# A decoder trunk on one core: where the second half's q is kept, and when its attention is queued

## The chip, the cores and the metric

One core of a Trainium2 chip runs the whole program. The metric is device time in microseconds (us) from launch to end. The engines are PE (TensorE, matmul and its weight loads), DVE (VectorE), ACT (ScalarE), POOL (GpSimd) and SP (SyncE, which here only issues DMAs). Each engine runs its instructions in the order in which they stand in its own queue; between engines they wait on semaphores.

## The reference

Two layers over x of 1024 tokens by 1024 features, float32. The first has the mixer that the change touches: one input projection feeds a sliding-window attention with rotary positions and a gated delta rule; both outputs, side by side, go through an output projection, and a layernorm and an MLP follow. The second layer has a recurrent mixer and the same MLP.

```python
def hybrid_mixer(x, w_in, sinks, conv_w, a_log, dt_bias, norm_w, w_out):
    proj = x @ w_in
    qa, ka, va, qkv_b, z, beta_logit, a_logit = split_cols(proj, HYB_SPLITS)
    qa = apply_rope(qa.reshape(bsz, T, A_Q_HEADS, A_HEAD_DIM))
    ka = apply_rope(ka.reshape(bsz, T, A_KV_HEADS, A_HEAD_DIM))
    o_a = sliding_window_attention(qa, ka, va, sinks)
    qkv_b = jax.nn.silu(causal_dwconv(qkv_b, conv_w))
    ...
    o_b = gated_delta_rule(qb, kb, vb, g, beta)
    ...
    return jnp.concatenate([o_a, o_b], axis=-1) @ w_out
for layer in range(DEPTH):
    x = layer_norm(DN_ALPHA * x + mix, ln1_g[layer], ln1_b[layer])
    x = layer_norm(DN_ALPHA * x + sqrelu_mlp(x, mlp_w1[layer], mlp_w2[layer]), ln2_g[layer], ln2_b[layer])
```

## The kernel before, in words

The 1024 tokens are two halves of 512 (`c` = 0 and 1, the first and the second half), each four tiles of 128 (`NT`). A float32 product is made of three matmuls in a reduced float32 format: every operand is kept as two parts, `h` (rounded) and `l` (what is left), and `mm3` adds h·h, h·l and l·h. Weights come by DMA to a staging tile `ws` and are split into `wh` and `wl` (`wblock`: a cast, mostly on ACT, and a subtract on DVE). Activations that are inputs of a product lie in an `ActT`: four tiles of 128x2048 for 512 features by 512 tokens each, two of parts h, two of parts l. `oT` is the `ActT` of the mixer's output; its features 0 to 511 (`quad(0, n)` for token tile n) are the attention's, the others (`oT.h(4 + h)`) those of delta head h.

The tiles of 128x2048 come from one pool of 14 (`gran`, ring `g`); `need("g", n)` holds a generator until n of them are free. There are smaller rings `t`, `s` and `f` of 128x512. PSUM has 8 banks: 4 for projections (`mm`), 4 for the small chains (`mx`).

The order of the program is made in Python by generators. `stream(c)` emits the heavy projections of half c: `hybrid` (the mixer's input projections: `kv_proj`, `q_proj`, and for delta head h `head_front` for k, q, v and `head_z` for the gate), `mix_out` (the output projection `out_proj`, with the layernorm behind it), `mlp_ln`, then the second layer. `mixers` is a list of small generators: `attn_preps` (rotary and transposes for one token tile after another), `attention` (scores, softmax, product with v), `head_mid` (the delta rule's chain of one head: four levels of a triangular solve in 32x32 blocks, then a scan over four token tiles), `layernorm`. The loop at the end keeps a clock of its own: when a mixer is due, it is advanced by a step, otherwise the current stream is, by one group of three matmuls. A stream that yields `UNIT` gives up its turn, and the loop picks again, the stream of lower phase first, the first half before the second; one that yields nothing special stays. PE's order is exactly the order in which the loop emits; the other engines' is made by a scheduler from it.

What matters around the change:
- `q_proj` puts q of half c into a tile of the pool, `st["qg"]`; `attn_preps` gives it back after its fourth `attn_prep`.
- `oT.quad(0, n)` takes the two tiles of the attention's output when it is first called, which `q_proj` does.
- The first half's `mix_out` needs two free tiles for the sums `yg`. `load_x(1)`, which loads and splits x of the second half, needs four.
- The second half's delta heads run one at a time: it has one ring, `t`.
- `mlp` takes the hidden blocks of the first layer in pairs of `straight` (4 blocks of 128 columns each) as long as the second half's `out_proj` has not begun, asked at every second one; from then on by `seven`, which makes a 2x2 block product with 7 products in place of 8, from sums of weights that POOL's and SP's DMAs prepare (`w2_sums`).

Of the kernel before, what the change touches and what calls it, by code (L numbers as in the profile page):

```python
# [13 lines left out]
ALU = mybir.AluOpType  # L14
# [6 lines left out]
CH = 512  # L21
# [27 lines left out]
BLOCK, UNIT = "block", "unit"  # L49
# [164 lines left out]
def trunk(ctx: ExitStack, tc, I, out):  # L214
    nc = tc.nc
    clk = Clock(tc, nc)
    V, G, S, PE = clk.engine(nc.vector, "V"), clk.engine(nc.gpsimd, "G"), clk.engine(nc.scalar, "S"), clk
# [14 lines left out]
    def nm(s):  # L232
        uid[0] += 1
        return f"{s}_{uid[0]}"
# [4 lines left out]
    def take(r, t):  # L239
        rings[r] -= 1  # L240
        assert rings[r] >= 0, r
        clk.tag[t.name] = r
        if spare[r]:
            old = min(spare[r], key=clk.touch)
            spare[r].remove(old)
            clk.reuse(t, old)
        return t

    def gran(dt=F32):
        return take("g", gpool.tile([P, 2048], dt, tag="g", name=nm("g")))  # L250
# [4 lines left out]
    def ts(r, dt=F32):  # L255
        return tl(r, dt)[:, :512]

    def free(r, *tiles):
        rings[r] += len(tiles)
        spare[r] += [t.name for t in tiles]  # L260
        assert rings[r] <= (GB if r == "g" else RINGS[r])

    def need(r, n=1):
        return wait(lambda: rings[r] >= n)
# [4 lines left out]
    def wait(cond):  # L269
        while not cond():  # L270
            yield BLOCK
# [4 lines left out]
    def mx_ps():  # L276
        return clk.tile("mx", 4, pmx.tile([P, 512], F32, tag="mx", name=nm("mx")))

    def v4(a):
        return a.rearrange("p (a b) -> p a b", a=4)  # L280
# [113 lines left out]
    def split_ps(h, l, ps):  # L394
        S.copy(h, ps)
        V.tensor_tensor(l, ps, h, ALU.subtract)
# [26 lines left out]
    def proj_tm(srcs, x, n, nk=KT, pre=None):  # L423
        ps = [mm_ps() for _ in range(NT)]
        for k2, src in enumerate(srcs):
            if pre is not None:
                pre(k2)
            wh, wl = wblock(src, 2 * n)
            for j in range(2):
                k = 2 * k2 + j  # L430
                for t in range(NT):
                    a, b = t * P, (t + 1) * P
                    mm3(ps[t][:, :n], x.h(k, a, b), x.l(k, a, b), wh[j], wl[j], k == 0, k == nk - 1)
                    if not (k == nk - 1 and t == NT - 1):
                        yield
        return ps
# [322 lines left out]

    def q_proj(c, x, st, oT):  # L760
        ps = yield from proj_tm([I["hin_q"][i] for i in range(4)], x, 512)
        st["qg"] = gran()
        for n in range(NT):
            oT.quad(0, n)
            S.copy(st["qg"][:, n * CH:(n + 1) * CH], ps[n])
        yield UNIT

    def kv_proj(c, x, st, oT, pre):
        ps = yield from proj_tm([I["hin_kv"][i] for i in range(4)], x, 264, pre=pre)
        st["ba"] = cpool.tile([P, NT, 8], F32, tag="ba", name=nm("ba"), bufs=2)  # L770
        st["k"] = []
        st["v"] = []
        for n in range(NT):
            kr = cpool.tile([P, P], F32, tag="kraw", name=nm("kraw"), bufs=5)
            v = cpool.tile([P, P], F32, tag="vraw", name=nm("vraw"), bufs=7)
            st["k"].append(kr)
            S.copy(st["ba"][:, n, :], ps[n][:, 256:264])
            S.copy(st["k"][n], ps[n][:, :128])
            S.copy(v, ps[n][:, 128:256])
            st["v"].append(v)  # L780
        yield UNIT

    def rope(x, src, ng, n, a, b):
        nh = x.shape[2] // 32
        cs, sn = (angles["t"].rearrange("p (s t d) -> p s t d", s=2, d=32)[:, k, n:n + 1, :].unsqueeze(1)
                  .to_broadcast([P, ng, nh, 32]) for k in range(2))
        av, bv = (z.rearrange("p (g h d) -> p g h d", g=ng, d=32) for z in (a, b))
        xv = src.rearrange("p g (h d) -> p g h d", d=32)
        V.tensor_tensor(av, xv, cs, ALU.mult)
        V.tensor_tensor(bv, xv, sn, ALU.mult)  # L790
        x4 = x.rearrange("p g (h s d) -> p g h s d", s=2, d=32)
        a4, b4 = (z.rearrange("p (g h s d) -> p g h s d", g=ng, s=2, d=32) for z in (a, b))
        V.tensor_tensor(x4[:, :, :, 0, :], a4[:, :, :, 0, :], b4[:, :, :, 1, :], ALU.subtract)
        V.tensor_tensor(x4[:, :, :, 1, :], a4[:, :, :, 1, :], b4[:, :, :, 0, :], ALU.add)

    def attn_prep(c, n, st, tl, o):
        q, kr = v4(st["qg"][:, n * CH:(n + 1) * CH]), st["k"][n]
        yield from need("f", 2)
        a, b, qs = tl[n % 2], ts("f"), v4(ts("f"))
        rope(kr.unsqueeze(1), kr.unsqueeze(1), 1, n, a[:, :128], b[:, :128])  # L800
        rope(qs, q, 4, n, a, b)
        yield at(kr, qs)
        ps = mx_ps()
        PE.transpose(ps[:, :P], kr, ident)
        kT = cpool.tile([P, P], F32, tag="kT", name=nm("kT"), bufs=4)
        V.tensor_copy(kT, ps[:, :P])
        ps = mx_ps()
        for g in range(4):
            PE.transpose(ps[:, g * P:(g + 1) * P], qs[:, g, :], ident)
        free("f", b, qs)  # L810
        S.copy(a, ps)
        o["qT"], o["kT"] = a, kT
        yield at(a, kT)
        o["ok"] = True
# [395 lines left out]
    def spawn(g, t=0.0):  # L1210
        mixers.append([lambda: t, g])

    def slots(n):
        slot["g"] = [gran() for _ in range(n // 4)]
        return [g[:, i * 512:(i + 1) * 512] for g in slot["g"] for i in range(4)]

    y2 = [dpool.tile([CH, D], F32, name=f"y2_{c}", tag=f"y2_{c}") for c in range(2)]
    st = [dict(), dict()]
    slot = dict(tl=None)

    def attn_preps(c, st, o):
        yield from wait(lambda: c == 0 or sts[0].get("att") == 4)
        angles["t"] = clk.tile("angles", 1, cpool.tile([P, 256], F32, tag="angles", name=nm("angles")))
        DA.dma_start(angles["t"], I["angles"][c])
        for n in range(NT):
            yield from wait(lambda: st.get("att", 0) >= n - 1)
            yield from attn_prep(c, n, st, slot["tl"], o[n])
        free("g", st["qg"])

    def attention(c, st, oT, o):  # L1230
        for n in range(NT):
            yield from attn_block(c, n, st, oT, slot["tl"], o[n])
            st["att"] = n + 1
        if c == 1:
            free("g", *slot["g"])
# [10 lines left out]
    def hybrid(c, x, oT, st, rs):  # L1246
        d = [dict() for _ in range(4)]
        if c == 0:
            slot["tl"] = slots(8)
            yield from kv_proj(c, x, st, oT, lambda k2: load_xT(c, x, k2))  # L1250
            DS.dma_start(csb, I["consts"])
        else:
            yield from wait(lambda: "x" in st)
            yield from head_front(c, 0, x, d[0], rs[0])
            yield from wait(lambda: sts[0].get("att", 0) >= 2)
            yield from kv_proj(c, x, st, oT, None)
        spawn(delta_scalars(c, st))

        def q():
            yield from need("g", 3)  # L1260
            yield from q_proj(c, x, st, oT)
            o = [dict() for _ in range(NT)]
            spawn(attention(c, st, oT, o))
            spawn(attn_preps(c, st, o))
        par = len(rs) > 1
        if not par:
            yield from q()
        for h in range(4):
            if h or par:
                yield from head_front(c, h, x, d[h], rs[h % len(rs)])  # L1270
            if not par and h:
                if h == 1:
                    yield from wait(lambda: "ln0" in sts[0])
                    yield from need("g", 2)
                yield from head_z(h - 1, x, oT, d[h - 1])
            yield from wait(lambda: h - st.get("scan", 0) < len(rs))
            spawn(head_mid(c, h, st, d[h], oT, rs[h % len(rs)]))
            if h == 1 and par:
                yield from q()
                yield from need("g", 2)  # L1280
                yield from head_z(0, x, oT, d[0])
                yield from head_z(1, x, oT, d[1])
                spawn(load_x(1, xTs[1]))
        if par:
            yield from head_z(2, x, oT, d[2])
        yield from head_z(3, x, oT, d[3])
        x.free()
        yield from wait(lambda: st.get("mids") == 4 and st.get("att") == 4)
# [215 lines left out]
```

## Time and profile before

| | |
|---|---|
| median of 3 runs | 2280.9 us (2277.67 to 2282.2) |
| the profiled execution | 2280.57 us, span 2278.7 us |
| mean granted clock of TensorE | 0.991 |
| instructions | 31,897 |
| first half's mixer, its input projections | to about 197 us |
| second half's kv and q projections | 245.3 to 290 us |
| first half's output projection | 365.0 to 425.1 us |

How to read it: busy time of PE overstates its pace, since matmuls overlap in the records; the distance between the starts of two neighbours is what one costs. In the tables of windows a column shows the busy time of an engine and how many of its instructions lie in the window; the granted clock is a share of full speed. In a timeline, the number in brackets is the engine's idle time before the row, and what ended it. Names such as `mm` and `mx` are PSUM tiles, `g`, `t`, `s`, `f` tiles of the rings; a matmul that reads `wh` or `wl` is a projection.

### The profile page before, as it was taken

To read this page: it belongs to the slowest core of one execution; us is meant where nothing else is said; L and a number is where in the kernel's file an instruction comes from. 1 tells how busy PE (TensorE), PEld (TensorE's weight loads), DVE (VectorE), ACT (ScalarE), POOL (GpSimd) and SP (SyncE) were. 2 spreads that over 40 slices of the span, in tenths; PEclk is the share of its full clock that TensorE was granted. 3 is DMA by queue.
4 is the path that set the end of the run, shared out by engine and by line. 5 is a ranking of instruction groups with operands and counts; after the bars stand their busy time and mean duration, and the time that the engine had idled before them with its cause. 6 is when DMAs were issued, how large, how long until landed. Compare 5 with 4: busy or idle time off the path is not lost.

```text
span 2278.7 us, 31897 instructions
## 1 busy us (share of the span) xinstructions
PE 2216.7 (97%) x12436; PEld 1790.4 (79%) x12436; DVE 1545.9 (68%) x2809; ACT 1049.1 (46%) x1874; POOL 28.9 (1%) x56
## 2 busy tenths in 40 slices
PE   8999989999999999999999999999999999999997
PEld 7767866778878887888888878878788887888886
DVE  7787684766645666596567898685565656776477
ACT  5465444434332344454344577373434444444442
POOL 0000000000000000000000000000000000000000
PEclk9999999999999999999999999999999999999999
DMA  4121221266778666677764343322533443454341
GB/s 165 61 78 39 94 67 45 74 175 178 216 213 225 196 211 200 210 241 229 226 216 149 128 138 105 136 79 97 180 107 121 139 148 123 155 166 148 120 163 69
DMA packets 87064, 332.22 MB, mean 146 GB/s; under 512 B 9600, under 2 KB 9984, under 8 KB 78720
## 3 DMA queue, kind: packets, MB, share of 16 engines
q1 hardware_dynamic: 73808, 275.32, 35.2%
q0 software_dynamic: 4608, 33.56, 7.8%
q10 hardware_dynamic: 8496, 21.30, 2.7%
q8 instruction: 97, 1.59, 0.3%
q14 instruction: 55, 0.45, 0.1%
HBM read 321.75 MB, written 75.50 MB: 174 GB/s over the span
## 4 chain that ended last, share of the span: by engine, by line
PE 85%; DVE 9%; ACT 3%; DMA 1%; issue 1%; ACTq 0%; DVEq 0%; SPq 0%
PE mm L206 66%; PE mx L206 17%; DVE g L178 3%; DVE wl L178 2%; PE mx L210 2%; DVE s L178 1%; DMA ws<-w 1%; ACT g L178 1%; ACT wh L178 1%; ACT s L178 1%; DVE t L178 1%; DVE f L178 1%; ACT f L178 0%; ACT t L178 0%; DVE lnw L178 0%
## 5 line engine op out<-in xcount | busy, mean ns | idle before, releaser
L206 PE MATMUL mm<-g,wh 128*128 128x512 f32 x2816 | 883.7, 395 | 3.6 <-DVE g L178 3.0
L178 DVE TENSOR_TENSOR wl<-ws,wh 128x1024 fp32r<-128x1024 f32 (+1 forms) x444 | 538.3, 1212 | 396.1 <-ACT wh L178 391.8
L178 ACT CAST wh<-ws 128x1024 fp32r<-128x1024 f32 (+1 forms) x356 | 371.5, 1044 | 705.8 <-PE mm L206 605.3
L206 PEld LDWEIGHTS mm<-g,wh 128*128 128x128 f32 x2816 | 521.6, 188 | 113.4 <-DVE g L178 5.1
L206 PE MATMUL mm<-g,wl 128*128 128x512 f32 x1408 | 549.5, 390 | 0.5 <-DVE wl L178 0.5
L206 PE MATMUL mm<-wh,s 128*128 128x512 f32 x1152 | 376.6, 393 | 0.7 <-DVE g L178 0.7
L206 PEld LDWEIGHTS mm<-g,wl 128*128 128x128 f32 x1408 | 264.7, 188 | 57.0 <-DVE wl L178 1.0
L206 PEld LDWEIGHTS mm<-wh,s 128*128 128x128 f32 x1152 | 216.3, 188 | 46.7 <-ACT s L178 1.1
L206 PE MATMUL mm<-wh,g 128*128 128x512 f32 (+1 forms) x768 | 239.3, 383 | 6.6 <-ACT wh L178 6.4
L206 PE MATMUL mm<-wl,s 128*128 128x512 f32 x576 | 224.3, 389 | 0.0
L206 PE MATMUL mx<-wh,s 128*128 128x512 f32 x576 | 187.8, 392 | 1.2 <-DVE s L178 1.2
L206 PEld LDWEIGHTS mm<-wh,g 128*128 128x128 f32 x768 | 143.0, 191 | 33.8 <-ACT wh L178 6.4
L178 ACT CAST s<-g 128x512 fp32r<-128x512 f32 x172 | 104.7, 622 | 105.2 <-PE mm L206 53.7
L178 DVE TENSOR_TENSOR s<-g,s 128x512 fp32r<-128x512 f32 x172 | 116.1, 685 | 44.7 <-ACT s L178 44.7
L206 PE MATMUL mm<-wl,g 128*128 128x512 f32 (+1 forms) x384 | 144.1, 375 | 0.2 <-DVE wl L178 0.2
L206 PEld LDWEIGHTS mx<-wh,s 128*128 128x128 f32 x576 | 108.1, 188 | 24.1 <-DVE s L178 2.0
L206 PEld LDWEIGHTS mm<-wl,s 128*128 128x128 f32 x576 | 108.3, 188 | 20.9
L206 PE MATMUL mx<-wl,s 128*128 128x512 f32 x288 | 112.1, 389 | 0.0
L178 DVE CAST wh<-ws 128x1024 fp32r<-128x1024 f32 x88 | 60.4, 686 | 73.0 <-PE mm L206 66.3
L178 DVE TENSOR_TENSOR g<-g,mm 128x512 f32<-128x512 f32 x136 | 89.1, 682 | 14.6 <-PE mm L206 14.2
L178 ACT ACTIVATE g<-mm 128x512 f32<-128x512 f32 x100 | 59.3, 593 | 73.0 <-PE mm L206 73.0
L206 PEld LDWEIGHTS mm<-wl,g 128*128 128x128 f32 x384 | 73.3, 191 | 11.7 <-DVE wl L178 0.6
(231 smaller groups left out, 2401.3 us busy)
## 6 DMA issues: line engine op xcount, KB each, us to landing
ws<-w SPq DMA_DIRECT2D x232, 512.0 KB, 3.3
ws<-t SPq DMA_DIRECT2D x96, 512.0 KB, 3.3
t<-w POOLq DMA_DIRECT2D x32, 1024.0 KB, 9.1
ws<-hin_fm SPq DMA_DIRECT2D x32, 512.0 KB, 3.3
t<-w SPq DMA_DIRECT2D x16, 1024.0 KB, 6.7
t<-t SPq DMA_DIRECT2D x16, 1024.0 KB, 6.5
ws<-rin SPq DMA_DIRECT2D x32, 512.0 KB, 3.3
ws<-hout SPq DMA_DIRECT2D x16, 512.0 KB, 3.4
```

The costliest lines, as they stand in the source:

```text
L178: r = f(*a, **k)
L206: ins = self.pe.matmul(out, lhsT, rhs, start=start, stop=stop, skip_group_check=fresh)
L210: return self._pe(self.pe.transpose(out, x, ident), out, [x], 0.00042 * 2 * out.shape[-1])
```

## The change

For the second half alone, q no longer gets a tile of its own. `q_proj` writes it as two parts, h and l, into the two tiles of `oT` that will take the attention's output of the same token tile; `attn_prep` adds them into its scratch tile and applies the rotary there. The second half's `q` then needs two free tiles, not three. For both halves, the `yield UNIT` at the end of `q_proj` goes, and a `yield UNIT` stands behind the spawn of each `head_mid`: attention, its preps and the delta head are in the list of mixers before the loop picks a stream again.

```diff
     def q_proj(c, x, st, oT):
         ps = yield from proj_tm([I["hin_q"][i] for i in range(4)], x, 512)
-        st["qg"] = gran()
+        g = st["qg"] = gran() if c == 0 else None
+        st["q"] = []
         for n in range(NT):
-            oT.quad(0, n)
-            S.copy(st["qg"][:, n * CH:(n + 1) * CH], ps[n])
-        yield UNIT
+            h, l = oT.quad(0, n)
+            if g is None:
+                split_ps(h, l, v4(ps[n]))
+                st["q"].append((h, l))
+            else:
+                S.copy(g[:, n * CH:(n + 1) * CH], ps[n])
+                st["q"].append(v4(g[:, n * CH:(n + 1) * CH]))
...
     def attn_prep(c, n, st, tl, o):
-        q, kr = v4(st["qg"][:, n * CH:(n + 1) * CH]), st["k"][n]
+        q, kr = st["q"][n], st["k"][n]
         yield from need("f", 2)
         a, b, qs = tl[n % 2], ts("f"), v4(ts("f"))
         rope(kr.unsqueeze(1), kr.unsqueeze(1), 1, n, a[:, :128], b[:, :128])
+        if c:
+            V.tensor_tensor(qs, *q, ALU.add)
+            q = qs
         rope(qs, q, 4, n, a, b)
...
-        free("g", st["qg"])
+        if c == 0:
+            free("g", st["qg"])
...
         def q():
-            yield from need("g", 3)
+            yield from need("g", 3 - c)
             yield from q_proj(c, x, st, oT)
...
             spawn(head_mid(c, h, st, d[h], oT, rs[h % len(rs)]))
+            yield UNIT
             if h == 1 and par:
                 yield from q()
```

The change is small, what it does to the order is not: the order is made by the loop, and from the first head on every choice can fall otherwise. Three places of it follow. The first is PE's queue behind the last matmul of the second half's q projection (`mm<-wh`). `mm_3370<-g` is `head_front` of delta head 1, the `mx` rows are the first steps of `head_mid` of head 0. Before:

```order
L206 MATMUL mm_3116<-wh_3317,g_2006 128x512
L206 MATMUL mm_3370<-g_2003,wh_3366 128x512
L206 MATMUL mm_3370<-g_2004,wh_3366 128x512
L206 MATMUL mm_3370<-g_2003,wl_3367 128x512
L210 MATMUL mx_3394<-csb,t_2285 128x128 x4
L210 MATMUL mx_3404<-csb,t_2578 128x128 x4
L206 MATMUL mx_3428<-t_3387,csb 128x512
```

Now, at the same place, with `mm_3431<-wh` and `mm_3432<-wh` the first half's `out_proj`:

```order
L206 MATMUL mm_3160<-wh_3326,g_2200 128x512
L210 MATMUL mx_3385<-csb,t_2592 128x128 x4
L210 MATMUL mx_3395<-csb,t_2789 128x128 x4
L206 MATMUL mx_3419<-t_3378,csb 128x512
L206 MATMUL mm_3431<-wh_3437,g_1079 128x512
L206 MATMUL mm_3431<-wl_3438,g_1079 128x512
L206 MATMUL mm_3431<-wh_3437,g_1080 128x512
L206 MATMUL mm_3432<-wh_3437,g_1079 128x512
```

The first half's `out_proj` moved up from 374 instructions behind that projection to 9 behind it; `head_front` of head 1 moved behind `out_proj`, and the first half's layernorm and the first block of its MLP follow it. From the end of `out_proj` to that first block PE's queue has 72 weight matmuls, where before, from the same to the same, it had 120.

The second place is PE's queue in the first half, where the triangular solve of its delta heads 2 and 3 (32x32 blocks, `t` of head 2 and `s` of head 3) lies beside its last attention tile and `head_front` of the second half (`mm_2292<-g`). Before, a piece of it:

```order
L206 MATMUL mx_2265<-t_1788 32x32 x16
L206 MATMUL mm_2292<-g_2003,wh_2288 128x512
L206 MATMUL mm_2292<-g_2004,wh_2288 128x512
L206 MATMUL mm_2292<-g_2003,wl_2289 128x512
L206 MATMUL mx_2253<-g_147,vraw_315 64x512
L210 MATMUL mx_2297<-csb,g_146 128x128 x2
L210 MATMUL mx_2297<-csb,g_147 128x128 x2
L206 MATMUL mx_2303<-t_1788 32x32 x16
```

Now, the end of the same stretch, up to the first matmul of that `head_front`:

```order
L206 MATMUL mx_2436<-s_2094 32x32 x16
L206 MATMUL mx_2454<-t_1765 32x32 x16
L206 MATMUL mx_2478<-t_1765 32x32 x16
L206 MATMUL mx_2497<-s_2094 32x32 x16
L206 MATMUL mx_2516<-t_1765 32x32 x16
L206 MATMUL mx_2534<-s_2094 32x32 x16
L206 MATMUL mx_2552<-t_1765 32x32 x16
L206 MATMUL mx_2571<-s_2094 32x32 x16
L206 MATMUL mm_2599<-g_2197,wh_2595 128x512
```

Where groups of three weight matmuls stood between the steps, 241 instructions in a row now have none; `head_front` of the second half begins 220 instructions later.

The third place is ACT's queue in the first half's MLP, behind its sixteenth hidden block (a `straight` has `r<-mm`, a block for `seven` has `g<-mm`; `lnw` rows are the second half's layernorm, `wh` casts are weights). Before:

```order
L178 ACTIVATE g_7179<-g_7179,lnw_7341 128x512 x3
L178 CAST wh_7624<-ws_7622 128x1024
L178 ACTIVATE g_7180<-g_7180,lnw_7341 128x512 x4
L178 ACTIVATE g_7553<-mm_7561 128x512
L178 ACTIVATE g_7553<-g_7553 128x512
```

Now:

```order
L178 CAST wh_7371<-ws_7369 128x1024
L178 ACTIVATE r_7250<-mm_7211 128x512
L178 ACTIVATE t_6576<-mx_7255,hsc_6574 128x128
L178 ACTIVATE r_7250<-r_7250 128x512
L178 CAST s_7197<-r_7250 128x512
```

Eight hidden blocks (two `straight`) more are made in full form, and one `seven` of the first layer's first half is gone: over the program, `mm<-wh,t` and `mm<-wl,t` products of 128x512 grow by 96, `mx<-wh,s` and `mx<-wl,s` fall by 72. On DVE there are 7 instructions fewer of 2812, on ACT 11 fewer of 1776, on SP's queue 6 DMAs fewer of 512; POOL has the same.

## What the change will do, predicted

> **What bounds the kernel now.** I read the page first, then the table of windows, then the timeline of PE in the two places that the change touches. The page says PE, and matmuls on streamed weights:
>
> ```profile
> PE 2216.7 (97%) x12436; PEld 1790.4 (79%) x12436; DVE 1545.9 (68%) x2809; ACT 1049.1 (46%) x1874; POOL 28.9 (1%) x56
> ...
> PE 85%; DVE 9%; ACT 3%; DMA 1%; issue 1%; ACTq 0%; DVEq 0%; SPq 0%
> ...
> L206 PE MATMUL mm<-g,wh 128*128 128x512 f32 x2816 | 883.7, 395 | 3.6 <-DVE g L178 3.0
> ```
>
> The 395 ns is one matmul's length; they overlap, so the price of one is the distance between two. The chain in order of time has long undisturbed pieces that give it:
>
> ```profile
> 810.93 5.44 PE mx L206 x24
> 816.38 16.32 PE mm L206 x72
> ```
>
> 5.44 / 24 = 0.227 us for one 128x512 matmul. Where PE runs at that distance, only fewer matmuls help. Where it doesn't, the windows tell (PE busy, weight loads, DVE, ACT, POOL, then the granted clock and the DMA share):
>
> ```profile
> core 0: us, PE busy (x) PEld busy (x) DVE busy (x) ACT busy (x) POOL busy (x), PEclk, DMA share, GB/s
> 197.00:223.00 26.00, 25.38 (x471) 16.73 (x469) 19.81 (x71) 10.32 (x38) 0.00 (x0) 1.00 0.07 16
> ...
> 317.00:365.00 48.00, 37.05 (x401) 22.34 (x386) 26.75 (x86) 20.82 (x58) 0.00 (x0) 0.79 0.17 56
> 365.00:425.00 60.00, 60.00 (x280) 42.48 (x280) 28.34 (x76) 26.57 (x70) 0.00 (x0) 1.00 0.19 62
> 425.00:470.00 45.00, 41.09 (x201) 33.66 (x200) 44.57 (x113) 25.55 (x57) 0.53 (x1) 0.92 0.26 94
> 470.00:702.00 232.00, 232.00 (x1922) 184.48 (x1921) 133.38 (x299) 88.75 (x193) 10.42 (x15) 1.00 0.72 203
> ```
>
> One stretch stands out: 317 to 365 us, PE idle for a fifth and the clock at 0.79. It is the second half's attention and first delta head with no weight matmul between their steps; the filler (`head_front` of head 1) is used up at 316.8, and the first half's `out_proj` comes only when `attn_preps` gives q's tile back. The timeline of PE shows it:
>
> ```profile
> 316.47 0.39 PE L206 MATMUL mm<-g,wl 128*128 128x512 f32 x1
> ...
> 318.07 0.45 PE L206 MATMUL mx<-t 32*32 32x32 f32 x32 [0.82 <-DVE t L178]
> 319.38 0.45 PE L206 MATMUL mx<-t 32*32 32x32 f32 x32 [0.86 <-DVE t L178]
> ...
> 340.91 1.08 PE L206 MATMUL mx<-t,t 64*64 64x64 f32 x8 [2.13 <-DVE asc L178]
> ```
>
> A triangular-solve step of a delta head takes 1.3 us from start to start when nothing lies between, though its PE work is 0.45. With `out_proj` as filler (365 to 425) the same sort of steps leave PE no idle at all.
>
> **The change, part by part.** The sum goes against the profiled execution's own 2280.57 us (span 2278.7); the median of the three runs, 2280.9, is 0.3 above it.
>
> *The bare stretch goes.* The program order has `out_proj` (192 matmuls, 43.5 us) start right behind the second half's q projection instead of 374 PE instructions later, and `head_front` of head 1 behind it: 264 weight matmuls now lie between the steps that had 72. What the stretch loses today is its idle, 48.00 - 37.05 = 10.95 us, and what the clock takes from the busy part, (1 - 0.79) x 37.05 = 7.8 us: 18.7 us. The least is the idle alone, 11; the most is 24, the 48 less what its 223 PE instructions take at the prices further down (8 products with v, 32 of scores, 46 transposes: 17.5 us, and some 6.5 for the 137 small ones). I take **-18.7**, since the two windows behind it, with filler, are at 60.00 of 60.00 and 232.00 of 232.00 at clock 1.00. `out_proj` is not lost as filler where it stood: the first half's MLP comes up behind it.
>
> On the clock, two slices of the stretch:
>
> ```profile
> 340.00:350.00 10.00, 7.27 (x31) 5.15 (x32) 4.30 (x14) 8.06 (x27) 0.00 (x0) 0.50 0.33 106
> 350.00:360.00 10.00, 8.71 (x35) 4.67 (x34) 1.84 (x5) 3.43 (x10) 0.00 (x0) 0.84 0.01 2
> ```
>
> The longest idle of PE shown in the stretch is 2.13 us, and yet the clock is halved for ten. The Trainium skill, page "TensorE: Matmul & The Clock Gate", section "Why this matters for your kernels", asks for no idle gap over about 3 us to keep the full clock. By that rule this stretch would never have lost its clock, and filling it would return 10.95 us alone; the trace speaks against the rule, since short idles suffice here.
>
> *One more piece of MLP in full form.* The first half's MLP does its hidden blocks in pairs of `straight` until the second half's `out_proj` has begun, then by `seven`, which has 7 products for 8. The second half's delta heads end later in the new order (its first has to share PE with `out_proj`), so six `straight` are done there instead of four. The activations `r<-mm`, four to each `straight`, count them:
>
> ```profile
> L178 ACT ACTIVATE r<-mm x28: 577/592/604, 473.5 to 2163.0; 128x512 f32<-128x512 f32 x28
> ```
>
> 28 are 7 blocks; the new program has 36. Over all, 128x512 weight matmuls grow by 96 and shrink by 72: 24 x 0.227 = **+5.4**. This is certain, PE being the bound there (232.00 of 232.00). DVE and ACT have slightly less to do, DMA six loads less; none of them bounds there.
>
> *The layernorm behind `out_proj` has less cover.* From 425 to 470 VectorE is busy for 44.57 of 45.00 us: it, not PE, sets the pace, and PE stands for it at the end, with a halved clock behind that:
>
> ```profile
> 461.92 1.71 PE L210 MATMUL mx<-csb,g 128*128 128x128 f32 x8 [2.25 <-DVE g L178]
> 463.30 0.80 PE L206 MATMUL mm<-g,wh 128*128 128x512 f32 x1
> 465.77 0.79 PE L206 MATMUL mm<-g,wh 128*128 128x512 f32 x1 [1.67 <-DVE g L178]
> ```
>
> In the new order VectorE's queue holds about as much from the last residual sum to the last split (112 instructions for 106; fewer of 1024 columns, more of 256: 40 us both, by the durations in this trace), but PE has 72 weight matmuls there for 120 (-10.9 us), and 43 more small ones of attention and delta. Their prices, where PE is not short of work (these rows have two records to a product with v and to a product of scores, one to a transpose):
>
> ```profile
> 330.61 1.07 PE L206 MATMUL mx<-g,vraw 128*64 128x512 f32 x2 [0.40 <-DVE g L178]
> 331.61 0.66 PE L210 MATMUL mx<-csb,g 128*128 128x128 f32 x4
> ...
> 333.94 1.16 PE L206 MATMUL mx<-kT,g 64*128 64x128 f32 x16
> ```
>
> Four products with v at 1.0 (330.61 to 331.61), sixteen of scores at 1.1 / 8 = 0.14 and the rest, 23, near 0.1 each: some 8.4 us. So PE waits 2.5 us longer, and one more where VectorE itself waits, since its queue now has attention steps between the layernorm's. I take **+3.5**. The least is 0 (the cover suffices), the most 11: four such waits of VectorE of about 2 us, as in the stretch above, on top of the 2.5.
>
> *A bare stretch in the first half.* The added yield also shifts the first half: its fourth `attn_prep` comes 78 matmuls later, so q's tile, still a tile of its own there, comes back later, x of the second half loads later, and `head_front` of the second half starts later. Now 241 PE instructions of the first half's attention and delta heads 2 and 3 stand with no weight matmul between; before, the same lay from 196.8 to 223.3 with 33 of them. The timeline there:
>
> ```profile
> 199.37 0.45 PE L206 MATMUL mx<-t 32*32 32x32 f32 x32
> 199.75 0.74 PE L206 MATMUL mm<-g,wh 128*128 128x512 f32 x2
> ...
> 218.44 0.45 PE L206 MATMUL mx<-t 32*32 32x32 f32 x32
> 218.72 0.48 PE L206 MATMUL mx<-s 32*32 32x32 f32 x32
> 219.12 0.73 PE L206 MATMUL mm<-g,wh 128*128 128x512 f32 x2
> ```
>
> The 33 take 7.5 us and will be done later, so the change costs T + 7.5 - 26.5 = T - 19, T being the time of the bare 241. At least 15 (26.5 less the 7.5 and about 4 of gaps): -4. At most 26.5 at full clock, as filler does not hasten a step: +7.5. Two heads alternate (tiles t and s), so one head's step covers part of the other's 1.3 us: I take 21.5, near the middle: **+2.5**.
>
> *The q itself.* Four casts in place of four copies on ACT, four subtracts more on DVE at its end, and four adds later, in the preps. The adds lie beside filler: 0. The subtracts release the four PSUM banks that `out_proj` wants next. On VectorE's queue they stand between rotary steps of the first two preps, each about 0.69:
>
> ```profile
> 288.72 0.69 DVE L178 TENSOR_TENSOR g<-s,g 128x512 fp32r<-128x512 f32 x1 [0.74 <-ACT g L178]
> 289.33 0.69 DVE L178 TENSOR_TENSOR g<-g,angles 128x512 f32<-128x512 f32 x1
> ```
>
> The last split ends some 5.4 us after the first begins; PE has 21 delta instructions and nine matmuls (about 5 us) before it needs that bank. **+0.6**, between 0 and 2. Queued behind, on SP, the eight `hout` loads pass three of `hin_fm`; on ACT's queue four loads of x pass; at a DMA share of 0.17 to 0.19 neither delays anything. POOL's sums of the second MLP weights begin earlier, and no reader of them moves forward by as much.
>
> *The sum:* -18.7 + 5.4 + 3.5 + 2.5 + 0.6 = -6.7, so 2280.57 - 6.7 = **2273.9 us**, say 2274. What stands behind 700 us is otherwise the same work with other neighbours: nothing, give or take 3.
>
> **Rivals.**
> 1. *The gap moves into the first half.* T is 26.5: the solve steps chain as slowly as before and nothing replaces the 33. Then -6.7 + 5 = -1.7: 2278.9. For it: 0.82 and 0.86 us of idle at each bare step. Against: two heads at once. Chance 0.17.
> 2. *VectorE takes over behind `out_proj`.* 11 instead of 3.5: +0.8, 2281.4. For it: 44.57 of 45.00. Against: its instructions there stay the same in number and length. Chance 0.10.
> 3. *Slower.* The first half's bare stretch goes as the second half's did: 48 us for 223 instructions, 0.215 each, would be 52 us for 241, with the clock down. The change is nil from T = 28.2 and 4.6 slower from 32.8; halfway between 26.5 and 52, T = 39, it gives -6.7 + 17.5 = +10.8: 2291.4. For it: the clock halved in a stretch that was 73% busy. Against: at 197 to 223 the clock is 1.00 and PE busy for 25.38 of 26.00. Chance 0.10.
> 4. *Only the idle is won.* If fillers mend the idle but not the clock, the first term is -10.95: +1.0, 2281.6. This is where the skill's rule on idle gaps leads as well. Against: clock 1.00 at 365 to 425 and 470 to 702, with such steps inside. Chance 0.06.
>
> That the change doesn't do what it says is ruled out by the order: `out_proj` stands where the first two preps are.
>
> **How the numbers follow.** The forecast has 0.57, its own range 2266 to 2277. All ends together would give 2258 to 2295 (-24 + 5.4 - 4 = -22.6, and -11 + 5.4 + 11 + 7.5 + 2 = +14.9); so many ends at once are unlikely, and 2265 to 2285 leaves out rival 3 and the tails. About 0.2% (4.6 us) is what a measurement of this kernel can tell from no change. Faster by more: nearly all of the forecast and a little of rival 1, 0.58. Within: most of rivals 1, 2, 4 and an edge of the forecast, 0.29. Slower: rival 3 and the tail of 2, 0.13.
>
> **What would show it.** Right: no window in the second half's attention with a clock under 0.95; 36 `r<-mm`; a stretch near 200 us without `mm` rows, of 20 to 23 us; PE's wait for DVE behind `out_proj` of 6 to 10 us. Wrong: that first stretch over 28 us or with a low clock; a wait for banks at `out_proj`'s first matmuls; a new idle of PE over 5 us behind 700 us, for which I have no term.

## The result, and the profile after

| | before | changed |
|---|---|---|
| median | 2280.04 us (4 runs, 2277.67 to 2282.2) | 2297.58 us (4 runs, 2293.12 to 2299.73) |
| span of the profiled execution | 2278.7 us | 2294.5 us |
| mean granted clock | 0.991 | 0.988 |

The ratio is 1.0075, with an interval of 1.0055 to 1.0094: slower by some 17 us, where 6.7 us of gain were forecast. The measured time lies above the forecast's range of 2266 to 2277 us.

The page of the changed kernel (busy time of the engines, the chain of waits by engine):

```profile
PE 2227.2 (97%) x12460; PEld 1799.1 (78%) x12460; DVE 1538.1 (67%) x2802; ACT 1040.9 (45%) x1863; POOL 28.7 (1%) x56
...
PE 87%; DVE 8%; ACT 3%; issue 1%; DMA 1%; DVEq 0%; ACTq 0%
```

and its instructions on the tiles `r`:

```profile
L178 ACT ACTIVATE r<-mm x36: 583/590/600, 428.5 to 2178.8; 128x512 f32<-128x512 f32 x36
```

The 36 activations are there as forecast. The shares of the whole span tell nothing of the loss; PE's even looks better on the chain. What tells is the table of windows (columns as before: time, PE busy, weight loads, DVE, ACT, POOL, granted clock, DMA share, GB/s), cut at the places that the prediction speaks of:

```profile
90.00:130.00 40.00, 35.85 (x429) 26.64 (x429) 24.04 (x77) 17.55 (x51) 0.20 (x2) 0.91 0.13 41
130.00:148.00 18.00, 17.75 (x116) 14.50 (x113) 9.76 (x36) 12.76 (x42) 0.00 (x0) 1.00 0.10 31
148.00:205.00 57.00, 48.80 (x261) 36.54 (x260) 51.97 (x150) 38.94 (x119) 0.40 (x4) 1.00 0.29 86
205.00:227.00 22.00, 17.33 (x463) 11.61 (x461) 17.09 (x65) 10.37 (x31) 0.00 (x0) 0.92 0.06 15
...
304.00:385.00 81.00, 80.78 (x678) 59.13 (x676) 58.49 (x174) 32.97 (x92) 0.00 (x0) 1.00 0.27 91
385.00:425.00 40.00, 31.32 (x151) 23.07 (x150) 31.67 (x75) 24.93 (x58) 0.94 (x1) 0.79 0.29 79
425.00:460.00 35.00, 34.91 (x183) 25.18 (x183) 17.60 (x55) 19.98 (x53) 0.82 (x1) 1.00 0.39 110
460.00:750.00 290.00, 287.69 (x2172) 226.59 (x2171) 173.15 (x368) 111.13 (x243) 12.45 (x17) 1.00 0.72 203
```

The bare stretch of the second half is gone: from 304 to 385 us PE is busy for 80.78 of 81.00 at full clock. Two other places have what it had. One is the layernorm behind `out_proj`, 385 to 425, with idle of 8.68 us and a clock of 0.79, the very clock of the old bare stretch. The other is the first half, ahead of all that the prediction looked at. The kernel before, in the same three first windows:

```profile
90.00:130.00 40.00, 39.03 (x465) 29.13 (x465) 30.13 (x97) 20.39 (x59) 0.20 (x2) 1.00 0.17 53
130.00:148.00 18.00, 17.36 (x104) 14.50 (x104) 14.55 (x47) 15.69 (x49) 0.10 (x1) 1.00 0.20 63
148.00:205.00 57.00, 51.44 (x331) 37.48 (x330) 48.41 (x135) 37.76 (x113) 0.30 (x3) 1.00 0.25 73
```

From 90 to 205 us PE was idle for 7.2 us; now it is for 12.6, and the clock falls to 0.91 in the first of the windows, which takes (1 - 0.91) x 35.85 = 3.2 us more. VectorE does 33.8 us of work from 90 to 148, where it did 44.7, and more behind: this fits work that PE needs coming later, and PE's waits from 90 to 205 us fit it too (what waits, for whom; total, times, longest). Before, the first two rows:

```profile
PE mx L210 <- DVE t L178: 3.4, 2, 2.0
PE mx L210 <- DVE s L178: 1.6, 1, 1.6
```

After, the first four:

```profile
PE mx L206 <- DVE s L178: 3.4, 3, 1.4
PE mx L210 <- DVE s L178: 3.2, 1, 3.2
PE mx L206 <- DVE t L178: 2.7, 2, 2.2
PE mx L210 <- DVE t L178: 1.6, 1, 1.6
```

Setting PE's timelines beside each other, at the same instructions of the program, places the difference (start of the instruction, us):

| | before | changed | later by |
|---|---|---|---|
| last weight matmul ahead of the first half's bare stretch | 196.6 | 204.5 | 7.9 |
| `head_front` of the second half, first | 199.8 | 227.0 | 27.2 |
| second half's q projection, last | 290.2 | 303.4 | 13.2 |
| second layer's first recurrent block, first | 1235.8 | 1248.0 | 12.2 |
| end of the span | 2278.7 | 2294.5 | 15.8 |

In both kernels the same 840 weight matmuls lie ahead of the end of q. So 13.2 of the 15.8 us are lost before the second half's attention begins, in a part of the program whose arithmetic the change leaves alone. Of what the second half was to give, 9.2 us by the terms of the sum that lie there (-18.7, +5.4, +3.5, +0.6), about 1 us remains at 1248, and 3.6 are lost later.

### The profile page after: what moved, and what is told of

Its sections match the earlier page's. It is cut to its first block, busy times and chain, and to the rows that moved or that the text cites. A ratio compares the mean times of both kernels' runs of the same rounds, so it can differ in the third digit from the quotient of the medians.

```text
span 2294.5 us, 31911 instructions
## 1 busy us (share of the span) xinstructions
PE 2227.2 (97%) x12460; PEld 1799.1 (78%) x12460; DVE 1538.1 (67%) x2802; ACT 1040.9 (45%) x1863; POOL 28.7 (1%) x56
## 4 chain that ended last, share of the span: by engine, by line
PE 87%; DVE 8%; ACT 3%; issue 1%; DMA 1%; DVEq 0%; ACTq 0%
PE mm L206 69%; PE mx L206 17%; DVE g L178 3%; PE mx L210 2%; DVE wl L178 2%; ACT g L178 1%; DVE s L178 1%; DVE t L178 1%; DVE f L178 1%; ACT wh L178 1%; DMA ws<-xT 0%; ACT s L178 0%; ACT t L178 0%; ACT f L178 0%; ACT L178 0%
## 5 line engine op out<-in xcount | busy, mean ns | idle before, releaser
L178 DVE TENSOR_TENSOR wl<-ws,wh 128x1024 fp32r<-128x1024 f32 (+1 forms) x438 | 530.6, 1212 | 396.5 <-ACT wh L178 383.1
L178 ACT CAST wh<-ws 128x1024 fp32r<-128x1024 f32 (+1 forms) x350 | 365.2, 1043 | 667.2 <-PE mm L206 574.8
L206 PE MATMUL mx<-wh,s 128*128 128x512 f32 x528 | 172.7, 392 | 1.8 <-DVE s L178 1.8
L178 ACT CAST s<-g 128x512 fp32r<-128x512 f32 x158 | 96.3, 622 | 100.3 <-PE mm L206 52.2
L178 DVE TENSOR_TENSOR s<-g,s 128x512 fp32r<-128x512 f32 x158 | 106.5, 685 | 40.0 <-ACT s L178 39.7
L206 PEld LDWEIGHTS mx<-wh,s 128*128 128x128 f32 x528 | 99.1, 188 | 23.1 <-DVE s L178 3.1
L178 DVE TENSOR_TENSOR g<-g,mm 128x512 f32<-128x512 f32 x144 | 95.1, 682 | 15.3 <-PE mm L206 14.7
L206 PE MATMUL mx<-wl,s 128*128 128x512 f32 x264 | 102.8, 389 | 0.0
L206 PE MATMUL mx<-g,wh 128*128 128x512 f32 x256 | 79.4, 391 | 0.0
```

The lines of the kernel that those rows point to most:

```text
L178: r = f(*a, **k)
L206: ins = self.pe.matmul(out, lhsT, rhs, start=start, stop=stop, skip_group_check=fresh)
```

## The experiments

All were timed in five rounds beside the kernel before (medians of 2279.0 to 2279.9 us, 15 to 23 runs).

**The two halves apart.** The change has two edits in one: the second half's q, and a yield moved for both halves. Run `e1_first_half_as_before` is the changed kernel with the first half's yields as they were:

```diff
+        if c == 0:
+            yield UNIT
...
             spawn(head_mid(c, h, st, d[h], oT, rs[h % len(rs)]))
-            yield UNIT
+            if c:
+                yield UNIT
```

> The changed kernel with the first half emitted as before (its yields stand where they stood), the second half as changed. By the two traces the first half's last common point, the end of the second half's q projection, came 13.2 us later in the changed kernel. Theory (the yield behind the first half's delta heads costs that): 2297.6 - 13 = 2284 us, within 4, and the second half's q projection ends near 290 us again. Rival (the loss is in the second half and the layernorm, the first half only drifted): over 2292 us.

Run `e2_first_half_alone` is the kernel before with nothing but the first half's yields moved:

```diff
-        yield UNIT
+        if c:
+            yield UNIT
...
             spawn(head_mid(c, h, st, d[h], oT, rs[h % len(rs)]))
+            if c == 0:
+                yield UNIT
```

> The kernel before with the changed places of the yields in the first half alone; q as before. Theory: the end of the second half's q projection comes 13 us later, at about 303 us, and the whole is 2280 + 13 = 2293 us, or a little less where what follows takes some of it up. Rival (drift that depends on the second half's change): within 3 us of 2280.

Measured: e1 2280.69 us, ratio 1.0012 (1.0003 to 1.0021); e2 2293.81 us, ratio 1.0069 (1.0057 to 1.0082). The product of the two ratios is 1.0081, within the changed kernel's interval. Both theories held. The first half's yields, not the q in parts, make the change slow; and the second half's edit, left alone, wins nothing either: e1 comes to the second layer's first block at 1233.4 us, 2.4 earlier than before, and its profiled execution still ends 2.0 later (2280.7).

**Which of the four moves.** In the kernel before, one at a time: e10 takes the yield from q's end and puts one behind the second head's start, where q begins; e11 and e12 take nothing away and add one behind the third and the fourth head's start (`h == 2` and `h == 3` in the last line but one).

```diff
-        yield UNIT
+        if c:
+            yield UNIT
...
             spawn(head_mid(c, h, st, d[h], oT, rs[h % len(rs)]))
+            if c == 0 and h == 1:
+                yield UNIT
```

> The kernel before with one of the first half's four moves alone: the yield at the end of q's projection is taken away and one stands behind the start of the second delta head, where q begins. The order then is that of the run of the first half alone up to the fourth head's front, nearly; the second half's front begins 124 TensorE instructions later than before (220 there). Theory, that the loss lies in the stretch from 95 to 165 us, which this one move sets: 8 to 12 us, about 2289 us. Rival, that the stretch without fillers at 205 us is the loss: less than half of the 14.5 us, 2284 us.

> The kernel before with a yield behind the start of the third delta head alone. Up to 148 us the order is that of before; the fourth attention prep comes 47 TensorE instructions later and the second half's front 188 later. Theory, that the stretch without fillers costs some 5 us: 2284 to 2286 us. Rival, that only the stretch from 95 to 165 us costs: 2280 us.

> The kernel before with a yield behind the start of the fourth delta head alone. The order differs from before only from 190 us on, and the second half's front comes 12 TensorE instructions later. Theory: within 2 us of before, 2280 us. Rival, that any other order than before's costs some us, wherever it differs: 2284 us or more.

Measured: e10 2290.9 us, 1.0047 (1.0033 to 1.0061); e11 2288.76 us, 1.0037 (1.0024 to 1.0049); e12 2281.77 us, 1.0004 (0.9995 to 1.0012). The theory of e10 and of e12 held; e11 cost some 9 us, where 4 to 6 were expected. The windows of e10:

```profile
90.00:130.00 40.00, 35.87 (x446) 26.79 (x444) 25.63 (x83) 17.56 (x51) 0.20 (x2) 0.96 0.12 41
...
205.00:232.00 27.00, 22.98 (x416) 15.38 (x414) 17.50 (x56) 12.64 (x35) 0.00 (x0) 0.87 0.04 12
```

and of e11:

```profile
90.00:130.00 40.00, 39.04 (x466) 28.99 (x465) 28.85 (x96) 19.33 (x56) 0.20 (x2) 1.00 0.12 41
...
148.00:205.00 57.00, 48.72 (x294) 36.32 (x293) 51.88 (x147) 39.66 (x118) 0.30 (x3) 0.99 0.28 90
205.00:232.00 27.00, 24.68 (x574) 15.49 (x577) 13.51 (x53) 11.49 (x33) 0.00 (x0) 0.90 0.01 3
```

e11 has the second of the changed kernel's two losses by itself, e10 has the first and a shorter form of the second. In e10 PE's last weight matmul ahead of the bare stretch stands at 205.2 us, 8.6 later than before (204.5 in the changed kernel); the next comes 18.5 us behind it, at a lowered clock, and q ends at 302.6, 12.3 later. In e11 nothing is lost up to 195.5 us; then come 213 PE instructions without a weight matmul, 24.4 us from the last one to the next, at a lowered clock, and q ends at 296.9, 6.7 us later than before. The two aren't parts of a sum: together they cost 20 us, and all four moves (e2) 14.5. And a yield alone needn't be harmful: e12, which changes the order from 190 us on but has only 37 such instructions, is the kernel before within its interval, though its q ends 2.2 us later.

**Two attempts on the first half that went the other way.** Run e6 has the yield behind the start of every head of the first half, and keeps the one at q's end:

```diff
             spawn(head_mid(c, h, st, d[h], oT, rs[h % len(rs)]))
+            if c == 0:
+                yield UNIT
```

> The kernel before with one unit of filler work more behind the start of each delta head of the first half, and q's own yield left where it was. Theory, that this one yield is the whole of the first half's loss (it changes when the mixers start, and with that all that follows): 2292 to 2294 us, as the run with both moves. Rival, that the loss needs q's missing yield too, or that it is a matter of which order happens to come out: 2280 us, or anything between.

Run e9 gives the first half's q the two parts as well, so that no q buffer of the first half holds up the second half's x:

```diff
-        g = st["qg"] = gran() if c == 0 else None
+        g = None
...
-        if c:
-            V.tensor_tensor(qs, *q, ALU.add)
-            q = qs
+        V.tensor_tensor(qs, *q, ALU.add)
+        q = qs
...
-            yield from need("g", 3 - c)
+            yield from need("g", 2)
```

> The changed kernel with the first half's q in two parts as well, so that the second half's input isn't held up by the first half's q buffer and the stretch of 241 TensorE instructions without a filler at 205 us goes. Theory, that this stretch costs 5 us of the first half's 13 and the rest is lost ahead of 205 us: about 2292 us. Rival, that the stretch is nearly all of it (its low clock included): 2284 us. Second rival, that the earlier load moves the loss elsewhere: 2297 us as the changed kernel, or more.

Measured: e6 2302.98 us, 1.01 (1.0087 to 1.0113), worse than both of its theories; e9 2301.2 us, 1.009 (1.0077 to 1.0103), its second rival. In e9 the bare stretch is gone (the second half's front begins 0.2 us behind the filler ahead of it), but that filler ends at 222.6 us instead of 204.5. A wait ahead of it has taken its place, here in PE's timeline of e9:

```profile
196.11 1.09 PE L210 MATMUL mx<-csb,s 128*128 128x128 f32 x4 [5.81 <-DVE asc L178]
```

So the stretch can't be priced by taking it out: where the fillers go earlier, the delta heads' steps lie barer elsewhere.

**The price of the two `straight` blocks.** Run e3 is the kernel before with six of them forced; e5 is e1 with four allowed again:

```diff
-        while e < 8 and not ((c == 1 or sts[1].get("op", -1) >= layer) and rings["g"] >= 2 and e % 2 == 0):
+        while e < 8 and not (e >= (6 if layer + c == 0 else 0) and (c == 1 or sts[1].get("op", -1) >= layer) and rings["g"] >= 2 and e % 2 == 0):
...
-        while e < 8 and not ((c == 1 or sts[1].get("op", -1) >= layer) and rings["g"] >= 2 and e % 2 == 0):
+        while e < 8 and not ((c == 1 or sts[1].get("op", -1) >= layer or (layer == 0 and e >= 4)) and rings["g"] >= 2 and e % 2 == 0):
```

> The kernel before, with six blocks in full form in the first half's first MLP in place of four: 24 matmuls more, nothing else in order ahead of them. Theory: 24 x 0.227 = 5.4 us, so 2285.5 us, within 2. Rival (the full form costs more than its matmuls, by other waits, or less, since its sums need less of VectorE): 8 us or more, or under 2 us.

> The run with the first half as before, and output heads 4 and 5 of the first half back among the fillers (four straight blocks instead of six). Theory, that the two blocks more cost what the run of six straight blocks in the kernel before cost (+7.2 us): 5 to 7 us under the first run, about 2274.5 us. Rival, that the fillers given to the later window are then lacking behind the output projection, where the attention's share of ScalarE and VectorE leaves TensorE bare: no gain, 2280 us.

Measured: e3 2286.52 us, 1.0039 (1.0026 to 1.0052), as expected. e5 2284.64 us, 1.0021 (1.0012 to 1.0029): 4 us above e1, whose interval it overlaps. So there is no gain, as the rival had it, though not for its reason, and its 2280 us were too low. A reason shows in the windows of e5,

```profile
800.00:860.00 60.00, 56.44 (x237) 46.16 (x236) 44.27 (x56) 28.98 (x42) 1.64 (x2) 0.94 0.64 187
```

and in its timeline of PE,

```profile
811.42 1.22 PE L206 MATMUL mx<-wh,s 128*128 128x512 f32 x2 [3.56 <-DVE s L178]
```

against e1's window:

```profile
800.00:860.00 60.00, 60.00 (x267) 49.69 (x266) 37.53 (x76) 23.71 (x33) 2.45 (x3) 1.00 0.58 178
```

Without the two blocks PE comes to the first `seven` at 804.5 us instead of 886.5, and stands there for the tiles `s`, which VectorE makes. The idle of 3.56 us with the lowered clock behind it, (1 - 0.94) x 56.44 = 3.4, take back more than the 5.4 us of matmuls.

**The layernorm behind `out_proj`.** Run e4 is e1 with the second half's attention held, from its third tile on, until the first half's layernorm is done:

```diff
         for n in range(NT):
+            if c == 1 and n >= 2:
+                yield from wait(lambda: 0 in normed)
             yield from attn_block(c, n, st, oT, slot["tl"], o[n])
```

(and its fourth prep likewise; `normed` is filled at the end of `layernorm`.)

> As e1_first_half_as_before, and the second half's third and fourth attention tiles wait until the first half's layernorm is through. In the changed kernel PE lost some 15 us between 385 and 425 us, where attention's VectorE and ScalarE work lies between the layernorm's. Theory (those queues, with the attention in them, hold the layernorm up): the loss there falls to the 7 us of before, and the whole is 8 us under e1. Rival (72 weight matmuls are too little cover, whatever the queues hold): the loss stays or grows, since PE has fewer small matmuls to do there, and the whole is that of e1 or above it.

Measured: 2275.42 us, 0.9988 (0.998 to 0.9997): 5.3 us under e1, where the theory had 8, and the intervals don't touch. It is also below the kernel before, by 0.7 to 4.6 us by its ratio's interval. The window of the layernorm in e1, then in e4:

```profile
385.00:425.00 40.00, 29.72 (x144) 22.56 (x143) 26.33 (x77) 21.32 (x59) 0.94 (x1) 0.83 0.34 92
...
385.00:425.00 40.00, 33.40 (x175) 26.01 (x174) 28.77 (x79) 24.63 (x63) 0.94 (x1) 0.91 0.34 98
```

Idle and lost clock are 6.6 + 3.0 = 9.6 us in e4, against 10.3 + 5.1 = 15.3 in e1 (and 8.7 + 6.6 = 15.3 in the changed kernel): 5.7 us less, close to the 5.3 of the medians. The 9.6 are not the 7 that the theory had. From 386.2 to 404.5 us PE has no weight matmul in e4 either, so that the rival's lack of cover may be what is left. Two runs tried to add to it. e8 puts four `straight` blocks in place of six (e5's line), e13 holds the third prep as well (`n >= 2` for the preps, which had `n >= 3`).

> The run with the second half's attention held behind the first half's layernorm, and four straight blocks instead of six. Theory, that the terms add: 5 to 7 us under the held run, about 2269.5 us, faster than the kernel before by 10 us. Rival, that the two blocks are needed as cover once attention is held: no gain over the held run, 2275 us.

> The held run with the second half's third attention prep held behind the layernorm as well (there it stood ahead of it), so that more of the second delta head's front is left to lie between the layernorm's instructions. Theory, that what is left of the layernorm's cost is attention's work on VectorE ahead of it: 3 us under the held run's 2275.4, about 2272.5 us. Rival, that the rest is the delta head's own steps: within 1.5 us of the held run.

Measured: e8 2276.48 us, 0.9985 (0.9974 to 0.9995), no gain over e4; it has e5's idle of 3.56 us at `seven` again, but at clock 1.00 from 800 to 860 us, so the wait explains 3.6 of the 5.4 us there, and what took the rest is not shown. e13 2278.7 us, 0.9997 (0.9988 to 1.0006), 3 us worse than e4, which neither its theory nor its rival had; in it the first delta head of the second half ends at 488.6 us instead of 472.0. Of all kernels run, e4 is with e8 the fastest.

## Why the prediction was wrong, point by point

The profiled execution came 15.8 us later, where 6.7 earlier were forecast. By the timelines these 22.5 us are 7.9 in the first half ahead of its bare stretch, 2.8 more than forecast in that stretch, 8.2 of the second half's gain that did not come (up to 1248 us), and 3.6 behind.

- **The bare stretch of the second half (-18.7): right that it goes.** 304 to 385 us is busy for 80.78 of 81.00 at clock 1.00.
- **What the sum had no term for: the first half ahead of its bare stretch, 7.9 us.** This is the first step that failed: a cost that was put at nothing without a reason. The prediction noted that the yield shifts the first half, and followed one consequence only, the late `head_front` of the second half. The order of delta heads 0 and 1, attention and fillers from 90 us on changes as well, without any long run lacking fillers, and was not gone through. e10 shows it with one head's move: its last filler stands at 205.2 us, 8.6 later than before.
- **The bare stretch of the first half (+2.5): the stretch was right, the term too small.** It takes 22.4 us from the last filler to the next, with 21.5 taken; by the prediction's own T - 19 that is 3.4, and up to the end of q it costs 13.2 - 7.9 = 5.3 us. What was missed is behind its last steps: the clock is still low as the weight matmuls begin, 0.50 from 227 to 230 us with PE busy throughout, which is 1.5 of the other 1.9. Here it is in PE's timeline, where two of them take 1.22 us (0.62 at 198.82 us, at full clock). A low clock in this stretch was one of the prediction's signs of failing.

```profile
225.96 0.65 PE L206 MATMUL mx<-t 32*32 32x32 f32 x32 [1.34 <-DVE t L178]
...
226.97 1.22 PE L206 MATMUL mm<-g,wh 128*128 128x512 f32 x2
```

- **The layernorm (+3.5): the mechanism was there, its size was off.** Idle and lost clock, by the windows, were 3.9 + 3.3 = 7.2 us before and are 15.3 now: +8.1. This is the second step that failed, by 4.6 us, though inside its own 0 to 11: the prediction weighed VectorE's work there (40 us both), found no more of it, and did not look at ScalarE's queue. What counts is whose work stands ahead of whose. The timelines of PE, DVE and ACT in that window:

```profile
396.28 0.68 PE L206 MATMUL mx<-t,t 128*128 128x128 f32 x4 [2.42 <-DVE asc L178]
...
408.92 0.45 PE L210 MATMUL mx<-csb,kraw 128*128 128x128 f32 x1 [1.86 <-DVE asc L178]
...
417.00 0.66 PE L210 MATMUL mx<-csb,g 128*128 128x128 f32 x4 [2.37 <-ACT t L178]
```

```profile
388.74 6.71 DVE L178 TENSOR_TENSOR g<-g,s 128x512 f32<-128x512 f32 x11
...
416.24 0.17 DVE L178 TENSOR_TENSOR asc<-asc 128x8 f32<-128x8 f32 x1 [2.69 <-ACT asc L178]
```

```profile
415.52 0.50 ACT L178 ACTIVATE g<-g,asc 128x256 f32<-128x256 f32 x1
...
416.58 0.37 ACT L178 ACTIVATE t<-mx,hsc 128x128 f32<-128x128 f32 x1
```

  Eleven residual sums stand on VectorE ahead of the attention's score reductions, for which PE then waits; and VectorE itself stands for 2.69 us for the softmax's eight exponentials on ScalarE, of which the first ACT row is the last, with layernorm work queued behind. PE's wait at 417.00 is for the `t` of the second ACT row, queued behind the exponentials. In e1, from which e4 is made, the loss is as large, but PE does not wait for `asc`; its two longest waits there are for `g` of ScalarE:

```profile
403.50 0.66 PE L210 MATMUL mx<-csb,g 128*128 128x128 f32 x4 [2.10 <-ACT g L178]
...
408.77 1.52 PE L206 MATMUL mm<-g,wh 128*128 128x512 f32 x2 [3.34 <-ACT g L178]
```

  The first stands behind eight exponentials, the second behind eight multiplications of the same softmax, 3.30 us on ScalarE. e4, which takes the attention's third tile out of there, has neither wait and gets 5.3 us back. So that attention in the layernorm's queues costs some 5 us is shown; that the residual sums do is read off the changed kernel's rows alone, and no run tests it.
- **The two `straight` blocks (+5.4): "certain" only in the old order.** Put there alone they cost 7.2 us (e3). In the changed order they cost nothing that shows: without them PE waits at `seven`, in e5 for more than they cost, in e8 for part of it.
- **Behind 700 us (nothing, give or take 3): +3.6 from 1248 us on**, a little over. With six `straight` blocks the second layer's order is another, with one idle that the prediction named as a sign of its failing:

```profile
1495.83 1.11 PE L210 MATMUL mx<-csb,g 128*128 128x128 f32 x4 [6.29 <-DVE g L178]
```

  All six kernels with six `straight` blocks that were profiled have the same idle, e1 and e3 without the first half's moves; none of those with four has it.
- **q itself (+0.6):** no run prices it alone. e4, with the q in parts and the attention held, comes to the second layer's first block at 1226.2 us, 9.6 earlier than before. Its layernorm costs +2.4 (9.6 for 7.2 before), so -18.7 + 5.4 + 2.4 = -10.9 leaves about 1 us for q and all else, if the other terms are right.
- **The rivals.** Rival 3, the slower one, named the right half of the program and half of the mechanism: it put the loss into the bare stretch at T = 39, which measured 22.4. Speaking against it was the clock of 1.00 there before; with 33 weight matmuls among the steps it stayed so, without them it went to 0.92 from 205 to 227 us (0.87 and 0.90 from 205 to 232 us in e10 and e11).

What stays open: some 4 us of the second half. The windows of bare stretch and layernorm with the 5.4 us of matmuls sum up to -5, the timelines give -1 (in e1 -2). No run takes the yield at q's end away without adding another, so e10's loss is not divided between the two, and the yield behind the first head's start has no run of its own. And why the loop of mixers chooses so much worse in the first half is not known: e6 and e9 show that the choice isn't mended by another yield or an earlier buffer.

## What to carry to other kernels

Where an order is made by a loop that chooses among ready pieces, a yield is an edit of the whole program behind it: go through the new order from its first difference on, and look at each engine that others wait for, not only at places where fillers are lacking. Split such a change into its edits before judging it; here the part that seemed incidental cost 14 us and hid that the other was nearly even. An equal amount of work on an engine is no equal wait: what matters is whose instruction stands ahead in its queue.

## What the runs showed of the hardware that had not been expected

- The clock falls in stretches whose idles are all short. In the changed kernel's layernorm (385 to 425 us) the longest idle of PE is 2.42 us and the mean granted clock is 0.79. The Trainium skill, page "TensorE: Matmul & The Clock Gate", section "Why this matters for your kernels", asks for no idle gap over about 3 us; by that row alone the clock would have stayed, and the trace disagrees, as it did in the old bare stretch. How much idle it takes is not shown: from 148 to 205 us the changed kernel is busy for 48.80 of 57.00 us at clock 1.00, e12 for 52.23 at 0.94. The layernorm and the bare stretches are also short of weight matmuls, and no run separates that from the idles.
- The loss in clock outlasts its cause: in the changed kernel it is 0.50 from 227 to 230 us, among the first weight matmuls behind the bare stretch, with PE busy for 3.00 of 3.00 us, so that a stretch costs more than its own length shows.
- The same two blocks cost 7.2 us in one order (e3 against before) and nothing in another (e1 against e5), with PE at 60.00 of 60.00 from 800 to 860 us in e3 and e1 alike: that PE is full doesn't show that its work may be taken away at its full price.
